# Delta rule: turning keys, queries, values and outputs with VectorE blocks and SBUF-to-SBUF DMAs instead of TensorE

## The chip, the cores and the metric

The kernel runs on one core of a Trainium2 chip. A core has a matrix engine (PE, with its weight loads as PEld), VectorE (DVE), ScalarE (ACT), GpSimd (POOL) and SyncE (SP). Each engine runs its own instructions in the order in which the program gives them, and waits in front of an instruction whose operands are not ready. SP and POOL issue the DMAs of this kernel. The metric is device time in microseconds; the kernel before took 1706.15 us, the median of three runs (1705.23 to 1707.87).

## The reference, cut to what matters

One decoder layer is computed for a prompt of 256 tokens and for 8 samples of 4 tokens, all in float32. Most of the arithmetic is in large projections (model width 2048, inner width 8192). Between them stands the gated delta rule with 8 heads of width 128, which the change is about:

```python
def l2norm(x):
    return x * lax.rsqrt(jnp.sum(x * x, -1, keepdims=True) + NORM_EPS)

qh, kh, vh = l2norm(q), l2norm(k), v            # (tokens, 8 heads, 128)
# in chunks of 64 tokens:
M    = where(strict, (k * beta) @ k.T * decay, 0)
T    = triangular_solve(eye + M, eye)
u    = T @ (v * beta)
w    = T @ (k * beta * exp(gcum))
attn = (q @ k.T) * decay
# over the chunks, with the state S (128 x 128 of each head):
v_new = u - w @ S
o     = (q * exp(gcum)) @ S + attn @ v_new
S     = S * exp(glast) + (k * exp(glast - gcum)).T @ v_new
o     = o * rsqrt(mean(o * o) + NORM_EPS) * gdn_norm_w * silu(z)
```

The samples take the same rule with chunks of 4 tokens and a given state each.

## The kernel before

**Blocks and turns.** All weights are streamed through SBUF in blocks of 512 KB. A block takes 24 matmuls: 8 weight tiles of 128 x 128, and three products each (`matmuls`, L206 to L208), since every float32 operand is split into a high and a low part. The main loop makes one turn for each block `i`, numbered from 0, and its program order is what counts below:

1. ACT writes the high part of block `i+3` (`split_hi`, L179). Its buffer is that of block `i-1`, so ACT waits here for the end of PE's matmuls of block `i-1`.
2. A generator of side work takes one step: `next(sgen)`, and then a step of the samples' generator `aux` where there is one. A `yield` in the code of the delta rule ends such a step. The step's instructions on all engines stand here in program order.
3. DVE writes the low part of block `i+3` (`split_lo`, L140, tile `lo`).
4. Pieces of evacuation that are due come next (for instance the short convolution, `w`, L265 to L287, or L318 to L334).
5. PE runs the 24 matmuls of block `i`.
6. SP issues the load of block `i+7` (`load`, L171, tile `raw`). Its buffer is free when DVE has written the low part of block `i+3`.

There are four buffers each of `raw`, `hi` and `lo`. The matmuls of block `i` need `hi` and `lo` of that block, which were written three turns earlier in program order.

**The delta rule** is side work, `gdn(G)` for the two halves `G` = 0 and 1 of four heads each; the first half begins in turn 20. For each half, keys and queries arrive with the head's width in the partitions (`kq`, `kqs` for samples). In order, `gdn` turns them by TensorE (L958, 16 transposes through the identity), sums squares for the norms (`ss`), turns the samples' keys and queries (L973, L974) and repeats the samples' keys four times (`four`, L976, then L980), computes the decays (`glx`, `gr`, L997; `E`), scales the turned keys (`kdec`), multiplies keys with keys and queries (L1030, L1031), and inverts the triangle: a small solve (`mx`, written by ACT and POOL at L1088 and L1089, used by PE at L1094), then three doublings (L1084). Then `U128`, a copy of the inverse by ACT (L1121), is ready; the values are turned by TensorE (L1219, 8 transposes) and the scan over four chunks begins (L1243, L1251, L1254, L1231). The samples run beside it (`sample`, L1139 to L1210), with repeated values at L1169 and L1176. At the end the outputs are turned (L1291, 8 transposes) and copied to `ao` by ACT.

`S0` holds the samples' states. POOL issues its loads at L926, ahead of all other work of the half. `S0` shares its place in SBUF with an earlier tile (tag `S0`).

**DMA order.** SP's DMAs are issued in program order. They take eight completion counters in turn, so that each waits for the DMA eight places before it to have landed.

## Time and profile before

| what | us |
|---|---|
| median of three runs | 1706.15 |
| span of the profiled execution | 1703.4 |
| PE busy in it | 1688.5 |
| DVE busy | 1007.2 |
| ACT busy | 734.1 |
| POOL busy | 133.8 |

The profiled execution has no time of its own beside its span; the median of the runs lies 2.75 us above that span, which holds what is before the first and after the last instruction.

The views are read in this way. A row of the waits gives the engine and line that waited, whom for, the sum in us, how often, and the longest. A row of the chain of waits, or of a timeline, starts with start and duration in us. A row of the groups ends in the sum in us, the mean in ns, and the idle time in front. A row of one source line gives least, median and greatest duration in ns. A row of the DMA issues gives the KB of one and the median time from issue to landing in us. "SPq" is SP issuing.

### The profile page before, as it was taken

The numbers are of one execution on the slowest core, as the hardware profiler recorded it, in microseconds if no ns is written. First come the engines' busy times: TensorE is split into PE (matmuls) and PEld (weight loads), VectorE is DVE, ScalarE is ACT, GpSimd is POOL, SyncE is SP. The second block draws the span as 40 slices with busy tenths as digits, with TensorE's granted clock in tenths as the row PEclk, the third lists the DMA queues.
The fourth block names the chain that finished last, engine by engine and source line by source line (L and its number), as shares of the span: only waits on it lengthen the run. The fifth ranks groups of instructions, "written<-read, shape, count | busy, mean of one in ns | idle before, by whom it ended". The sixth has DMA issues, their size and how long they took to land.

```text
span 1703.4 us, 31106 instructions
## 1 busy us (share of the span) xinstructions
PE 1688.5 (99%) x13063; PEld 1668.7 (98%) x13063; DVE 1007.2 (59%) x1296; ACT 734.1 (43%) x1067; POOL 133.8 (8%) x223
## 2 busy tenths in 40 slices
PE   9999999999999999999999999999999999999997
PEld 7999999999999999999999999999999999999997
DVE  5577876758544444456778844566445654466565
ACT  4675626333543333334445533444334433344442
POOL 2232412023300000000010000000000000000000
PEclk9999999999999999999999999999999999999999
DMA  8464456435555555555565555555555555555552
GB/s 244 140 194 139 123 175 200 150 115 180 162 170 169 166 162 170 163 164 165 158 190 174 165 170 161 164 170 162 167 168 161 163 171 162 164 167 164 162 162 80
DMA packets 275097, 279.18 MB, mean 164 GB/s; under 512 B 13131, under 2 KB 270092, under 8 KB 274952
## 3 DMA queue, kind: packets, MB, share of 16 engines
q1 hardware_dynamic: 270414, 265.95, 51.3%
q0 software_dynamic: 4256, 11.12, 2.3%
q8 instruction: 102, 1.67, 0.4%
q14 instruction: 37, 0.30, 0.1%
q10 hardware_dynamic: 288, 0.13, 0.0%
HBM read 269.68 MB, written 7.48 MB: 163 GB/s over the span
## 4 chain that ended last, share of the span: by engine, by line
PE 98%; DVE 1%; DMA 0%; POOL 0%; issue 0%; SPq 0%; ACT 0%; POOLq 0%; ACTq 0%
PE acc L206 31%; PE acc L208 31%; PE acc L207 31%; PE g L1084 1%; DMA xr<-in_x_prompt_dram 0%; PE g L1072 0%; PE g L1231 0%; PE g L1251 0%; PE g L831 0%; DVE w L143 0%; PE g L1254 0%; PE g L1203 0%; PE g L1243 0%; PE g L608 0%; PE g L798 0%; PE g L958 0%
## 5 line engine op out<-in xcount | busy, mean ns | idle before, releaser
L140 DVE TENSOR_TENSOR lo<-raw,hi 128x1024 fp32r<-128x1024 f32 (+2 forms) x502 | 614.0, 1226 | 556.2 <-ACT hi L179 553.7
L179 ACT CAST hi<-raw 128x1024 fp32r<-128x1024 f32 (+1 forms) x498 | 517.6, 1041 | 765.0 <-PE acc L207 707.7
L206 PE MATMUL acc<-xh,hi 128*128 128x288 f32 x1408 | 422.9, 300 | 0.0
L208 PE MATMUL acc<-xh,lo 128*128 128x288 f32 x1408 | 416.7, 296 | 0.0
L207 PE MATMUL acc<-xl,hi 128*128 128x288 f32 x1408 | 416.5, 296 | 0.0
L206 PE MATMUL acc<-dh,hi 128*128 128x290 f32 x1024 | 303.9, 297 | 0.0
L207 PE MATMUL acc<-dl,hi 128*128 128x290 f32 x1024 | 303.3, 296 | 0.0
L208 PE MATMUL acc<-dh,lo 128*128 128x290 f32 x1024 | 302.7, 296 | 0.0
L206 PE MATMUL acc<-hh,hi 128*128 128x288 f32 x1024 | 302.3, 295 | 0.0
L208 PE MATMUL acc<-hh,lo 128*128 128x288 f32 x1024 | 302.3, 295 | 0.0
L207 PE MATMUL acc<-hl,hi 128*128 128x288 f32 x1024 | 302.3, 295 | 0.0
L206 PEld LDWEIGHTS acc<-xh,hi 128*128 128x128 f32 x1408 | 265.4, 189 | 2.6 <-issue 0.7
L207 PEld LDWEIGHTS acc<-xl,hi 128*128 128x128 f32 x1408 | 265.8, 189 | 0.5
L208 PEld LDWEIGHTS acc<-xh,lo 128*128 128x128 f32 x1408 | 265.6, 189 | 0.0
L206 PEld LDWEIGHTS acc<-dh,hi 128*128 128x128 f32 x1024 | 193.6, 189 | 0.1
L208 PEld LDWEIGHTS acc<-dh,lo 128*128 128x128 f32 x1024 | 193.3, 189 | 0.0
L207 PEld LDWEIGHTS acc<-dl,hi 128*128 128x128 f32 x1024 | 193.3, 189 | 0.1
L207 PEld LDWEIGHTS acc<-hl,hi 128*128 128x128 f32 x1024 | 192.5, 188 | 0.0
L208 PEld LDWEIGHTS acc<-hh,lo 128*128 128x128 f32 x1024 | 192.3, 188 | 0.0
L206 PEld LDWEIGHTS acc<-hh,hi 128*128 128x128 f32 x1024 | 192.1, 188 | 0.0
L207 PE MATMUL acc<-ml,hi 128*128 128x288 f32 x256 | 75.6, 295 | 0.0
L208 PE MATMUL acc<-mh,lo 128*128 128x288 f32 x256 | 75.6, 295 | 0.0
(404 smaller groups left out, 1620.0 us busy)
## 6 DMA issues: line engine op xcount, KB each, us to landing
raw<-in_w_in_dram SPq DMA_DIRECT2D x176, 512.0 KB, 3.5
raw<-in_w_up_dram SPq DMA_DIRECT2D x128, 512.0 KB, 3.9
raw<-in_w_down_dram SPq DMA_DIRECT2D x128, 512.0 KB, 3.7
raw<-in_w_o_dram SPq DMA_DIRECT2D x32, 512.0 KB, 3.7
raw<-in_w_a_out_dram SPq DMA_DIRECT2D x16, 512.0 KB, 3.7
raw<-in_w_b_out_dram SPq DMA_DIRECT2D x16, 512.0 KB, 3.6
S<-in_state_gdn_dram POOLq DMA_DIRECT2D x8, 512.0 KB, 7.8
out_dram<-S POOLq DMA_DIRECT2D x8, 512.0 KB, 4.9
```

What stands on the lines that cost most here:

```text
L140: dve.tensor_tensor(out=out, in0=a, in1=b, op=op)
L179: act.copy(his[i][:, k:k + step], raw[i][:, k:k + step])
L206: pe.matmul(o, wh, xh_, start=st, stop=False)
L207: pe.matmul(o, wh, xl_, start=False, stop=False)
L208: pe.matmul(o, wl, xh_, start=False, stop=en)
L1084: pe.matmul(out[r, q * 64:q * 64 + 64], a[r, q, :], b[r, q, :], start=True, stop=True)
```

## The change

For each half, the 16 + 2 + 4 + 8 + 8 transposes by TensorE and the 4 products that repeat the samples' values are replaced:

- Keys, queries and the samples' keys and queries are turned in blocks of 32 x 32 within their partitions by `dve.transpose` (tiles `tk` and `ts`), and the blocks are then moved to other partitions by DMAs from SBUF to SBUF, which SP issues: 16 to `spk`, 16 to `kr` (the samples' keys repeated), 16 to `kT` and 16 to `qT`.
- The squares for the norms are taken from the moved tiles, in one piece of 1024 for keys and one for queries; `kdec` is scaled from `kT`.
- The values are turned by DVE (`tv`) and moved by 16 DMAs to `v`, ahead of the triangle's inversion. The transposes stand in a step of their own.
- `tk`, `qT`, `kT` and `tv` lie in the place of `S0`; the loads of `S0` are issued after the moves of `v`.
- The samples' values are copied by ACT (`Xs`) and repeated by 16 DMAs (`v4`).
- The outputs are turned by DVE (`to`) and moved to `ao` by 32 DMAs.
- The `yield` between the copy of `U128` and the scan is gone; two more stand in `sample`; one of two is gone ahead of the outputs' turn.

This is 128 DMAs of 8 to 32 KB for each half, all on SP's queue, between the loads of the weights.

```diff
-        S0 = pl.tile([P, 4, 8, P], F32, tag="S0", name=nm("S0"))
-        for hh in range(4):
-            gps.dma_start(S0[:, hh], A["state_gdn"][0, :, 4 * G + hh].rearrange("b d e -> d b e"))
...
-        for c in range(4):
-            kt = gtile()
-            kv = kt.rearrange("p (h c) -> p h c", h=4)
-            for hh in range(4):
-                pe.transpose(kv[:, hh, :], kq[:, hh, c].rearrange("p s x -> p (s x)"), ident)
...
-            dve.tensor_reduce(out=red[:, c, :], in_=s2, axis=mybir.AxisListType.X, op=ADD)
-            if c % 2:
+        flat = T([P, 4096], "S0")
+        tk = flat[:, 0:2048].rearrange("p (j a c r x) -> p j a c r x", j=4, a=2, c=4, r=2)
+        qT = flat[:, 2048:3072].rearrange("p (i c r x) -> p i c r x", i=4, c=4, r=2)
+        kT = flat[:, 3072:4096].rearrange("p (i c r x) -> p i c r x", i=4, c=4, r=2)
+        tv = flat[:, 0:1024].rearrange("p (j c r x) -> p j c r x", j=4, c=4, r=2)
...
+        for hh in range(4):
+            dve.transpose(out=tk[:, :, hh % 2, :, hh // 2],
+                          in_=kq[:, hh].rearrange("p c s x -> p c (s x)").rearrange("p c (j b) -> p j c b", j=4))
+            if hh == 1:
+                dve.transpose(out=ts.rearrange("p u h x -> p (u h x)"), in_=kqs.rearrange("p u h b t -> p (u h b t)"))
+            if hh % 2:
                 yield
+        for i in range(4):
+            for n in range(4):
+                sp.dma_start(spk[rows32(n), :, rows32(i)], ts[rows32(i), :, n])
+                sp.dma_start(kr[rows32(n), :, rows32(i)], ts[rows32(i), 0])
         tt(gl, bc(G_["g"][:, :, pr], 64),
            cst("lc").unsqueeze(1).unsqueeze(1).to_broadcast([P, 4, 2, 64]), MUL)
...
+        yield
+        for i in range(4):
+            for j in range(4):
+                sp.dma_start(kT[rows32(j), i], tk[rows32(i), j, j // 2])
+                sp.dma_start(qT[rows32(j), i], tk[rows32(i), j, 1 - j // 2])
         yield
...
+        for u in range(2):
+            act.activation(junk, spk[:, u], AF.Square, accum_out=ss[:, 16 + u:17 + u])
+        act.activation(sqr[:, 0:512], kr.rearrange("p h d -> p (h d)"), AF.Square)
+        dve.tensor_reduce(out=ss[:, 18:22], in_=sqr[:, 0:512].rearrange("p (h d) -> p h d", h=4),
+                          axis=mybir.AxisListType.X, op=ADD)
+        yield
+        for u, t in enumerate((kT, qT)):
+            s2 = sqr.rearrange("p (q i x) -> p i q x", q=8, i=4)
+            act.activation(s2, t.rearrange("p i c r x -> p i (c r) x"), AF.Square)
+            dve.tensor_reduce(out=ss[:, 8 * u:8 * u + 8], in_=sqr.rearrange("p (q d) -> p q d", q=8),
+                              axis=mybir.AxisListType.X, op=ADD)
         yield
...
+        while cur[0] < mark["kqv_end", G] + 3:
+            yield
+        for r in range(2):
+            dve.transpose(out=tv[:, :, :, r],
+                          in_=vf[:, r].rearrange("p c a x -> p c (a x)").rearrange("p c (j b) -> p j c b", j=4))
+        yield
+        v = T([P, 4, 4, 2, 32], "v")
+        for i in range(4):
+            for j in range(4):
+                sp.dma_start(v[rows32(j), i], tv[rows32(i), j])
+        S0 = T([P, 4, 8, P], "S0")
+        for hh in range(4):
+            gps.dma_start(S0[:, hh], A["state_gdn"][0, :, 4 * G + hh].rearrange("b d e -> d b e"))
...
+            act.copy(Xs, pv_[:, 0:P])
             act.mul(vns, pv_[:, 0:P], sc[:, 1:2])
...
+            for hh in range(4):
+                for n in range(4):
+                    sp.dma_start(v4[rows32(n), hh], Xs[rows32(hh)])
...
+        to = T([P, 4, 4, 2, 32], "kdec")
...
+        for j in range(4):
+            for i in range(4):
+                h0 = 4 * G + 1 - i // 2
+                t0 = gd["ao"][rows32(j), 1, h0:h0 + 3:2, 0:NP_].rearrange("p r (c n x) -> p n r c x", c=4, n=2)
+                for r in range(2):
+                    sp.dma_start(t0[:, i % 2, r], to[rows32(i), j, :, r])
```

How the order of the instructions moves is shown at three places, all in the first half.

SP at the first moves, before (only the loads of weights) and now. `kso` and `kr` are the moved samples' tiles (`spk` lies in the place of `kso`), `S_1125` is the flat tile with `tk`, `kT` and `qT`:

```order
L171 DMA raw_1111<-in_w_in_dram 128x4x256
L171 DMA raw_1186<-in_w_in_dram 128x4x256
L171 DMA raw_1244<-in_w_in_dram 128x4x256
L171 DMA raw_1287<-in_w_in_dram 128x4x256
L171 DMA raw_1328<-in_w_in_dram 128x4x256
```

```order
L171 DMA raw_1211<-in_w_in_dram 128x4x256
L966 DMA kso_1127<-U_1126 32x2x32
L967 DMA kr_1128<-U_1126 32x4x32
...
L171 DMA raw_1278<-in_w_in_dram 128x4x256
L973 DMA S_1125<-S_1125 32x256
L974 DMA S_1125<-S_1125 32x256
...
L171 DMA raw_1340<-in_w_in_dram 128x4x256
L171 DMA raw_1388<-in_w_in_dram 128x4x256
```

The first "..." stands for 30 more rows of the pair above it, the second for 30 more as well: 32 DMAs now stand between the loads of blocks 28 and 29 and 32 between those of blocks 29 and 30.

DVE over the same turns, now. The reductions of `ss` read squares that ACT takes from the moved tiles:

```order
L140 TENSOR_TENSOR glx_1344<-gl_1122,glx_1344 128x512
L983 TENSOR_REDUCE ss_1123<-vmh_1116 128x4
L140 TENSOR_TENSOR lo_1351<-raw_1169,hi_1342 128x1024
L143 SCALAR_TENSOR_TENSOR w_1353<-w_1353,hw 128x312 x3
L989 TENSOR_REDUCE ss_1123<-vmh_1116 128x8 x2
L140 TENSOR_TENSOR lo_1396<-raw_1211,hi_1390 128x1024
```

The two rows of `lo` are the low parts of blocks 27 and 28. They stand behind the reductions, in turns 24 and 25. Before, the reductions of `red` stood in turns 20 and 21 and that of `ss` in turn 23, each behind a square of what TensorE had turned.

POOL at the small solve, before and now. `S` is `S0`, `b` the spread keys, `mx` the operand of the small solve on PE:

```order
L273 COPY stB<-w_1588 128x27
L1065 COPY b_1120<-kqs_424 128x8x4 x4
L1089 ISA
L1089 TENSOR_TENSOR mx_1631<-xt_1538,mx_1631 128x512
L265 MEMSET w_1706 128x3
```

```order
L273 COPY stB<-w_1608 128x27
L1054 DMA S_1699<-in_state_gdn_dram 128x8x128 x4
L1075 COPY b_1115<-kqs_424 128x8x4 x4
L1099 ISA
L1099 TENSOR_TENSOR mx_1709<-xt_1558,mx_1709 128x512
L265 MEMSET w_1750 128x3
```

The four loads of `S0` have moved from the head of the half to the place just ahead of `mx`. The first of them writes where the moves of `v` read.

More of the change, by code (lines that the diff above doesn't have):

```diff
@@ L913, in gates, with rows32 @@
         yield
[L916 to L917 removed]
+    def rows32(n):
+        return slice(32 * n, 32 * n + 32)
     def gdn(G):
@@ L948, in gdn @@
         ss = T([P, 22], "ss")
-        red = T([P, 4, 4], "red")
         kdec = T([P, 4, 2, P], "kdec")
@@ L952, in gdn @@
         rows = (slice(0, 64), slice(64, 128))
-        for c in range(4):
-            kt = gtile()
-            kv = kt.rearrange("p (h c) -> p h c", h=4)
-            for hh in range(4):
-                pe.transpose(kv[:, hh, :], kq[:, hh, c].rearrange("p s x -> p (s x)"), ident)
-            s2 = sqr[:, 512 * (c % 2):512 * (c % 2) + 512].rearrange("p (h c) -> p h c", h=4)
-            act.activation(s2, kv, AF.Square)
-            for par in range(2):
-                act.copy(kdec[rows[par], c], kv[rows[par], par::2, :])
-            dve.tensor_reduce(out=red[:, c, :], in_=s2, axis=mybir.AxisListType.X, op=ADD)
-            if c % 2:
+        flat = T([P, 4096], "S0")
@@ L965, in gdn @@
                 yield
+        for i in range(4):
+            for n in range(4):
+                sp.dma_start(spk[rows32(n), :, rows32(i)], ts[rows32(i), :, n])
+                sp.dma_start(kr[rows32(n), :, rows32(i)], ts[rows32(i), 0])
         tt(gl, bc(G_["g"][:, :, pr], 64),
            cst("lc").unsqueeze(1).unsqueeze(1).to_broadcast([P, 4, 2, 64]), MUL)
-        ssv = ss[:, 0:16].rearrange("p (a c r) -> p a c r", a=2, c=4)
-        for par in range(2):
-            act.copy(ssv[rows[par], 0], red[rows[par], :, par::2])
-            act.copy(ssv[rows[par], 1], red[rows[par], :, 1 - par::2])
@@ L972, in gdn @@
-        sp2 = gtile()
-        pe.transpose(sp2[:, 0:128], kst, ident)
-        pe.transpose(sp2[:, 128:256], qst, ident)
-        gps.tensor_copy(wide, four(kst))
-        yield
-        ktr = gtile()
-        for hh in range(4):
-            pe.transpose(ktr[:, hh * P:hh * P + P], rep4[:, hh * P:hh * P + P], ident)
-        kr = T([P, 4, P], "kr")
-        for u in range(2):
-            act.activation(junk, sp2[:, u * P:u * P + P], AF.Square, accum_out=ss[:, 16 + u:17 + u])
-        act.copy(kr, ktr.rearrange("p (h d) -> p h d", h=4))
@@ L1020, in gdn @@
         act.activation(Ef, Ef, AF.Exp)
-        kdf = kdec.rearrange("p c r x -> p (c r) x")
-        tt(kdf, kdf, bc(qc(kdr), P), MUL)
+        tt(kdec.rearrange("p c r (i x) -> p i (c r) x", i=4), kT.rearrange("p i c r x -> p i (c r) x"),
+           bc(bmid(qc(kdr), 4), 32), MUL)
         yield
@@ L1168, in sample @@
             yield
-            act.copy(wide, four(Us))
             yield
@@ L1185, in sample @@
             done.append(1)
+            yield
+            yield
+            vr = sqr[:, 0:512].rearrange("p (h d) -> p h d", h=4)
+            tt(vr, v4, bc(rsc[:, 1], P), MUL)
+            v3 = pl.tile([P, 4, P], F32R, tag="U", name=nm("v3"))
+            lows(v3, vr, 1)
             vm = {}
@@ L1242, in gdn @@
             for p in range(2):
-                pe.matmul(p2[:, p * P:(p + 1) * P], U128[:, 2 * c + p, :], v[:, c, p, :], start=True, stop=True)
-            tt(v[:, c], p2[:, 0:256].rearrange("p (r x) -> p r x", r=2), bc(brk[:, c, :], P), MUL)
+                pe.matmul(ix(p2[:, p * P:(p + 1) * P]), U128[:, 2 * c + p, :], v[:, :, c, p], start=True, stop=True)
+            tt(v[:, :, c].rearrange("p i r x -> p r i x"), p2[:, 0:256].rearrange("p (r i x) -> p r i x", r=2, i=4),
+               bc(bc(brk[:, c, :], 4), 32), MUL)
             yield
@@ L1250, in gdn @@
                 r = rows[hh % 2]
-                pe.matmul(p3[hh % 2][:, hh // 2, :], kdec[r, c, hh // 2, :], v[r, c, hh // 2, :],
+                pe.matmul(ix(p3[hh % 2][:, hh // 2, :]), kdec[r, c, hh // 2, :], v[r, :, c, hh // 2],
                           start=True, stop=True)
             for p in range(2):
-                pe.matmul(p4[:, p * P:(p + 1) * P], aT[:, 2 * c + p, :], v[:, c, p, :], start=True, stop=True)
+                pe.matmul(ix(p4[:, p * P:(p + 1) * P]), aT[:, 2 * c + p, :], v[:, :, c, p], start=True, stop=True)
             p4v = p4[:, 0:256].rearrange("p (r x) -> p r x", r=2)
```

48 lines of the change are left out of this document (13 added, 35 removed).

## Prediction

> **What bounds the kernel now.** I read the page first, then the waits, then the chain that ended last.
>
> ```profile
> span 1703.4 us, 31106 instructions
> PE 1688.5 (99%) x13063; PEld 1668.7 (98%) x13063; DVE 1007.2 (59%) x1296; ACT 734.1 (43%) x1067; POOL 133.8 (8%) x223
> ACT hi L179 <- PE acc L207: 707.7, 369, 4.4
> SPq L171 <- DVE lo L140: 1373.9, 475, 9.1
> PE g L1203 <- DVE E L143: 3.0, 1, 3.0
> ```
>
> PE sets the time, and inside the program it stands still once, for 3.0 us. ACT waits for PE, SP for DVE: these run ahead of PE by three blocks and are held back by its buffers. So every matmul taken away is worth its time, and any wait that eats the lead of three blocks is paid in full. The chain gives PE's pace at the places of the change:
>
> ```profile
> 92.99 0.87 PE g L958 x8
> 97.06 0.87 PE g L958 x8
> 121.35 0.27 PE g L1030 x4
> 123.41 0.33 PE acc L206
> 139.54 0.47 PE g L1094 x2
> 180.11 0.87 PE g L1219 x8
> 201.15 0.89 PE g L1176 x8
> 279.08 0.87 PE g L958 x8
> 325.62 0.47 PE g L1094 x2
> ```
>
> Eight transposes take 0.87 us. From 93.86 to 97.06 runs block 20: 3.20 us for 24 matmuls, 0.133 each. The products of turn 28 take 2.06 (121.35 to 123.41).
>
> **What the change removes.** For each half 38 transposes, 38/8 x 0.87 = 4.1, and the repeated values, 0.89: 5.0 us, 10.0 for both. All of it is on the bounding engine and is gained. ACT's and DVE's savings gain nothing by themselves.
>
> **What it adds on SP.** Each half gets 128 DMAs in SP's queue. What an issue costs, and how long it takes to land:
>
> ```profile
> L171 SPq DMA_DIRECT2D raw<-in_w_in_dram x176: 367/368/544, 2.2 to 733.0; - x176
> L779 SPq DMA_DIRECT2D xr<-in_x_sample_dram x4: 464/465/910, 1.7 to 8.1; - x4
> 19.59 0.33 SPq L1351 DMA_DIRECT2D lnr<-in_ln_b_dram  x1
> 19.97 0.32 SPq L1352 DMA_DIRECT2D lnr<-in_gdn_norm_w_dram  x1
> L748 SPq DMA_DIRECT2D out_dram<-r x2: 717/860/1004, 1698.5 to 1699.2; - x2
> cf<-in_cf_dram SPq DMA_DIRECT2D x1, 64.0 KB, 2.0
> out_dram<-Y SPq DMA_DIRECT2D x4, 256.0 KB, 2.7
> xr<-in_x_sample_dram SPq DMA_DIRECT2D x4, 64.0 KB, 8.9
> ```
>
> A 512 KB load costs SP 0.37 us and a half-KB one 0.32, so size hardly matters; from 19.59 to 19.97 one follows the other with 0.05 between. No SBUF-to-SBUF DMA is in this trace. Bounds: 0.37 us for each (0.32 + 0.05), and 0.51 (0.465 + 0.05, `xr` from L779, the same 32 partitions); 0.86 was seen where two queues issued at once. I take 0.41, the steady load and the gap. Landing: 2.0 is the least, 2.7 for stores out of SBUF, 8.9 at the crowded start. I take 2.0, the nearest in size. So 32 moves hold SP for 13.1 us, 16 for 6.6, and a moved tile lands 2 us behind its last issue.
>
> [...]
>
> Other durations:
>
> ```profile
> L179 ACT CAST hi<-raw 128x1024 fp32r<-128x1024 f32 x492 | 514.2, 1046 | 761.7 <-PE acc L207 707.7 <-issue 41.4 <-ACT hi L179 8.6
> L140 DVE TENSOR_TENSOR lo<-raw,hi 128x1024 fp32r<-128x1024 f32 x492 | 608.7, 1239 | 552.6 <-ACT hi L179 550.2
> L963 DVE TENSOR_REDUCE red<-vmh 128x4 f32<-128x512 f32 x8 | 5.5, 686 | 8.2 <-ACT vmh L960 8.2
> L1114 DVE STREAM_TRANSPOSE xt<-U 128x512 f32<-128x512 f32 x4 | 2.8, 712 | 0.1
> L140 DVE TENSOR_TENSOR kdec<-kdec,kdr 128x1024 f32<-128x1024 f32 x2 | 2.4, 1215 | 0.0
> 117.13 0.29 DVE L1001 RECIPROCAL rn<-nr 128x22 f32<-128x22 f32 x1 [1.26 <-ACT nr L1000]
> ...
> 118.88 0.69 DVE L140 TENSOR_TENSOR E<-E,cf 128x512 f32<-128x512 f32 x1
> ...
> 122.91 0.68 DVE L140 TENSOR_TENSOR gl<-E,nbr 128x512 f32<-128x512 f32 x1
> ...
> 125.09 1.39 DVE L140 TENSOR_TENSOR aT<-g,E 64x512 f32<-64x512 f32 x2
> ...
> 127.65 1.70 DVE L143 SCALAR_TENSOR_TENSOR w<-w,hw 128x312 f32<-128x312 f32 x3
> ```
>
> So: `hi` 1.05, `lo` 1.24, a reduction of 512 0.69 and of 1024 about 1.2 (`lo`, of equal size), two turned tiles of 512 1.42, `kdec` 1.2, the group from `rn` to `E` 2.44 (117.13 to 119.57), from `gl` to `aT` 3.57 (122.91 to 126.48), the convolution 1.70.
>
> **First half, the moves of keys.** Turn 20 starts at 93.0 as before; without transposes turns 21 to 25 start 3.20 apart, 96.2 to 109.0.
>
> - Turn 21: `hi` to 97.3, two turned tiles behind the convolution to 98.5, `lo` to 99.7, then SP's load to 100.1. The 32 moves of turn 22 end 13.1 later at 113.2; the last, issued at 112.8, lands at 114.8. The load of block 29 ends at 113.6. The 32 moves of keys and queries end at 126.7; the last of the keys is issued at 125.9 and lands at 127.9, the queries 0.4 later, hidden.
> - Turn 24: ACT squares `kr` (0.6) to 115.4, DVE reduces to 116.1, the low part of block 27 follows at 117.3. PE has started turn 27 at 115.9 (112.2 + 0.47 of L997 + 3.20) and wants the low part after two matmuls, at 116.2: it stops for 1.1.
> - Turn 25: square of keys 1.05, reduction 1.2, square of queries into the same scratch 1.05, reduction 1.2, then the low part of block 28, 1.24: 127.9 + 5.8 = 133.7. PE starts turn 28 at 120.2, does 2.06 of products and two matmuls, and stops at 122.5: 11.2 us.
> - Turns 29 to 33: DVE is now what PE follows. Its low parts are ready at 139.1 (1.70 + 2.44 + 1.24), 141.5, 146.3 (3.57 + 1.24), 149.2 and 153.6 (1.70 + 1.42 + 1.24); PE's turns start at 136.7, 142.0, 145.2, 149.2, 152.4: it stops for 2.1, 0, 0.8, 0 and 0.9.
>
> The late loads of blocks 29 and 30, queued behind the moves, land by 117.2 and 130.7 and are not what is late.
>
> **First half, the small solve.** POOL's rows:
>
> ```profile
> 85.66 3.60 POOL L926 DMA_DIRECT2D S<-in_state_gdn_dram  x4
> 128.32 2.25 POOL L1065 COPY b<-kqs 128x32 f32<-128x32 f32 x4
> 135.91 1.55 POOL L1089 TENSOR_TENSOR mx<-xt,mx 128x512 fp32r<-128x512 f32 x1 [5.34 <-ACT mx L1088]
> ```
>
> In turn 31 SP's 16 moves of `v` follow the load at 154.0; the last is issued at 160.2 and lands at 162.2. POOL's first load of `S0` waits for that, since `tv` lies there. Behind it on POOL stand three more loads, the copies and `mx`: 3.6 + 1.7 (four copies, 2.25 in this row beside a busy DVE, so I take less) + 1.55 gives 169.1. PE comes to the small solve, turn 34, at 156.5 and stops for 12.6. Before, the loads of `S0` waited for nothing and were issued long ahead; this cover is gone.
>
> The half's stops: 1.1 + 11.2 + 2.1 + 0.8 + 0.9 + 12.6 = 28.7.
>
> **Second half.** It starts one turn earlier, behind the 32 moves of the outputs, which hold SP until 5.9 us after its start; with three loads behind them the first moves begin at 7.5. `kr` lands at 22.2, `kT` at 35.3. The convolutions are missing on DVE. The same steps give low parts at 25.0 (block +7, PE wants it at 23.1), 41.0 (+8, wanted at 30.3), then stops of 0.6 and 0.6; `v` lands at 64.5, `mx` is ready at 70.9, and PE is there at 61.3. Stops: 1.9 + 10.7 + 0.6 + 0.6 + 9.6 = 23.4.
>
> **The missing step ahead of the scan.** ACT's copy of `U128` and PE's first product with it now stand in one turn:
>
> ```profile
> 180.01 1.05 ACT L179 CAST hi<-raw 128x1024 fp32r<-128x1024 f32 x1 [2.39 <-PE acc L207]
> 180.96 1.24 ACT L1121 COPY U<-U 64x512 f32<-64x512 f32 x2
> ```
>
> PE is free at 180.11 and the copy ends at 182.20: 2.1 us of standing for each half, 4.2.
>
> **PE's pace after a long stop.** At the start of the trace matmuls follow each other more slowly:
>
> ```profile
> 11.02 0.66 PE L798 MATMUL g<-cf,xr 128*128 128x128 f32 x2 [0.45 <-DMA xr<-in_x_prompt_dram]
> ...
> 19.47 0.44 PE L207 MATMUL acc<-xl,hi 128*128 128x288 f32 x1
> 19.71 0.44 PE L208 MATMUL acc<-xh,lo 128*128 128x288 f32 x1
> ```
>
> 0.24 against 0.133, and this holds from PE's last stop at 11.02 until 19.95 at least: 8.9 us of which 8.9 x (1 - 0.133/0.24) = 4.0 are lost. Whether a stop of ten us brings that back, no row shows; the bounds are 0 and 4.0 for each long stop. After the moves of keys it costs nothing, since DVE and POOL set what follows. After the small solve I take the middle, 2 us for each half, 4 in all. [...]
>
> **Costed at nothing.** The 16 moves of `v4` (6.6 + 2.0) have two turns and more than 8 us until `vr`. The moves of outputs delay one weight load by 13 us; it has 7 us until ACT wants it and 7 more until PE does. New strides of the scan's operands move the same elements. The stop of 3.0 at L1203 may go or grow, as POOL's order changes: 3 either way.
>
> **The sum.** -10.0 + 28.7 + 23.4 + 4.2 + 4 = +50.3. The span becomes 1703.4 + 50.3 = 1753.7; the median of the runs lies 2.75 above the profiled span, so **1756 us**.
>
> The bounds: 80 issues lie on each half's two chains, 160 in all; at 0.37 they give -6, at 0.51 +16. Six landings at 2.7 give +4. The pace gives -4 or +4, L1203 -3 or +3. The likeliest case's own range is 1743 to 1783.
>
> **The rivals.**
>
> - *Cheap issues: faster.* If an SBUF-to-SBUF move cost SP at most 0.1 us, 64 would take 6.4, the keys would land at 108 and all low parts would be in time; POOL would have `mx` 13.1 us after the start of turn 30 (2.6 to the load, 1.6 + 2.0, 3.6, 1.7, 1.55), just as PE comes. Then only -10.0 + 4.2 is left, 1700 us. It decides from about 0.2 us: 127.9 - 11.2 = 116.7 is when the keys must land. Against it: no issue of SP in these rows is under 0.32. [...] 6%.
> - *Only the keys' moves bite.* If the moves of `v` land and POOL gets through before PE comes, the stops of 12.6 and 9.6 and the 4 of pace fall away: 1730. For it: POOL's rows are rough, and its first load might be let go by the first of the moves that free its place; against it, it would have to come 12.6 us sooner. 13%.
> - *Slow moves.* With eight in flight, a landing of 5 us sets a pace of 5/8 = 0.63: 160 x 0.22 + 6 x 3 = 53 more, about 1809. For it: the 8.9 of the crowded start and the 0.86 of L748; against it, both rows are of moments when many DMAs stood in line, and 64 KB landed in 2.0. 9%.
>
> **How the numbers follow.** The forecast holds 70%; 2% remain for a change that cancels to nothing. Predicted 1756, range 1728 to 1785: it takes in the second rival and leaves out the first and the third and what lies past the bounds. A measurement of this kernel tells 0.2% (3.4 us) from no change. Faster: 8% (the first rival, and some unseen gain); same 3%; slower 89%.
>
> **What would show it.** Right: SP's moves at 0.37 to 0.51 a piece; DVE's `ss` waiting for ACT and ACT for DMA by ten us; PE's longest waits at L208 for `lo` and at the small solve for POOL's `mx`, some 10 us each, twice; 2 us at the first product of the scan. Wrong: moves issued in 0.1 us, or PE busy through turn 28, or `mx` ready before PE.

## The result, and the profile after

The changed kernel takes **1829.7 us** (median of four runs, 1828.8 to 1830.2) against 1705.7 for the kernel before beside it: a ratio of 1.072, 95% interval 1.0704 to 1.0735. The sign was forecast, the size was not: 1756 was predicted, and 1829.7 lies 45 us above the range. The profiled execution has a span of 1828.4, 125.0 more than before and 74.7 more than the sum of the prediction (1753.7).

The page of the changed kernel, its span, PE, and PE's granted clock in 40 slices:

```profile
span 1828.4 us, 31220 instructions
PE 1703.5 (93%) x12971; PEld 1677.5 (92%) x12971; DVE 1013.1 (55%) x1308; ACT 724.2 (40%) x1029; POOL 128.0 (7%) x221
PEclk9987999868998999999999999999999999999999
```

PE stands for 6% of the span, and in the slices of the delta rule the clock falls to 0.6 to 0.8, where all slices of before show 9. Its waits, with the sum, the number and the longest, in us:

```profile
PE acc L208 <- DVE lo L140: 41.6, 8, 16.2
...
PE g L1250 <- ACT U L1131: 4.3, 2, 2.1
PE g L1250 <- DVE v L143: 2.5, 6, 1.1
```

All rows of this view add up to 117.4 us, against 7.1 before: 110.3 us of new stops. Eight of them are long. In the timeline of PE (start, duration, instruction; in brackets how long PE had stood, and for whom):

```profile
126.41 0.61 PE L208 MATMUL acc<-xh,lo 128*128 128x288 f32 x1 [10.11 <-DVE lo L140]
148.56 0.61 PE L206 MATMUL acc<-xh,hi 128*128 128x288 f32 x1 [15.41 <-ACT w L268]
187.75 0.80 PE L1104 MATMUL g<-mx,bo 128*128 128x512 f32 x1 [14.14 <-POOL mx L1099]
...
350.49 0.61 PE L206 MATMUL acc<-xh,hi 128*128 128x288 f32 x1 [10.23 <-ACT hi L179]
...
373.84 0.61 PE L208 MATMUL acc<-xh,lo 128*128 128x288 f32 x1 [12.62 <-DVE lo L140]
398.04 0.61 PE L208 MATMUL acc<-xh,lo 128*128 128x288 f32 x1 [16.21 <-DVE lo L140]
431.65 0.80 PE L1104 MATMUL g<-mx,bo 128*128 128x512 f32 x1 [12.12 <-POOL w L318]
572.10 0.61 PE L206 MATMUL acc<-xh,hi 128*128 128x288 f32 x1 [9.84 <-ACT hi L179]
```

The first three are the first half: behind the 32 moves to `spk` and `kr`, behind the 32 of keys and queries, and at the small solve. The next four are the second half, the first of them behind the first half's 32 output moves. The last stands behind the second half's output moves. Each is longer than forecast, or was not forecast. The way from the moves to the first two stops of a half is the forecast one: ScalarE's squares wait for the moves (L981 for the keys' row copy `kr` and `kso`, L988 for keys and queries), and VectorE's sums and the low parts `lo` stand behind them. ScalarE's waits, the sum, number and longest over both halves:

```profile
ACT vmh L988 <- DMA S<-S: 37.7, 2, 19.3
ACT vmh L981 <- DMA kso<-U: 32.0, 2, 16.5
```

Why they are longer stands in the rows of SP's issues, one source line each (least, median and greatest duration of one issue in ns):

```profile
L171 SPq DMA_DIRECT2D raw<-in_w_in_dram x176: 367/368/796, 2.2 to 857.8; - x176
L966 SPq DMA_DIRECT2D kso<-U x32: 585/599/1673, 100.5 to 368.6; - x32
L1051 SPq DMA_DIRECT2D v<-S x32: 512/589/1562, 169.8 to 423.6; - x32
L1304 SPq DMA_DIRECT2D ao<-kdec x64: 585/599/1615, 323.4 to 566.2; - x64
```

A load of weights costs SP 0.37 us in the median as before, though one right behind moves took 0.53 (at 122.39). A move from SBUF to SBUF costs 0.59 to 0.60, with the 0.05 to the next one **0.64 us**, where the prediction took 0.41. It landed 1.8 to 1.9 us after its issue, where the prediction took 2.0.

The second difference is PE's pace. Windows of PE in the changed kernel (width, PE's busy time with the number of matmuls begun, granted clock, DMA share, GB/s), each 8 us from the end of a long stop:

```profile
148.60:156.60 8.00, 6.52 (x33) 0.68 0.25 74
187.75:195.75 8.00, 8.00 (x48) 0.78 0.78 221
...
398.00:406.00 8.00, 7.96 (x44) 0.70 0.49 138
```

The clock is 0.68 to 0.78, and 33 to 48 matmuls are begun in 8 us. What is left of the span's growth, 125.0 - 110.3 + 10.0 = 24.7 us, I put down to this pace. It is a remainder, not a measurement: summed over PE's busy time up to 600 us, the granted clock falls short of 1.0 by 20.7 us, so that some 21 of the 24.7 are shown and the other 3 to 4 stay open.

### The profile page after: what moved, and what is told of

The parts are those of the page before. It is cut to its first block, busy times and chain, and to the rows that moved or that the text cites. A ratio compares the mean times of both kernels' runs of the same rounds, so it can differ in the third digit from the quotient of the medians.

```text
span 1828.4 us, 31220 instructions
## 1 busy us (share of the span) xinstructions
PE 1703.5 (93%) x12971; PEld 1677.5 (92%) x12971; DVE 1013.1 (55%) x1308; ACT 724.2 (40%) x1029; POOL 128.0 (7%) x221
## 3 DMA queue, kind: packets, MB, share of 16 engines
q0 software_dynamic: 4256, 11.12, 2.2%
## 4 chain that ended last, share of the span: by engine, by line
PE 81%; SPq 8%; DVE 4%; DMA 2%; issue 2%; POOL 1%; ACT 1%; POOLq 0%; DVEq 0%; ACTq 0%
PE acc L206 26%; PE acc L207 26%; PE acc L208 26%; SPq L1304 2%; DVE lo L140 2%; DMA raw<-in_w_in_dram 1%; SPq L1051 1%; SPq L974 1%; SPq L1187 1%; SPq L966 1%; SPq L973 1%; SPq L967 1%; PE g L1094 1%; DMA xr<-in_x_prompt_dram 0%; PE g L1082 0%
## 5 line engine op out<-in xcount | busy, mean ns | idle before, releaser
L208 PE MATMUL acc<-xh,lo 128*128 128x288 f32 x1408 | 425.0, 302 | 41.7 <-DVE lo L140 41.6
L206 PE MATMUL acc<-xh,hi 128*128 128x288 f32 x1408 | 429.9, 305 | 35.5 <-ACT hi L179 20.1
L207 PE MATMUL acc<-xl,hi 128*128 128x288 f32 x1408 | 423.5, 301 | 0.0
L208 PEld LDWEIGHTS acc<-xh,lo 128*128 128x128 f32 x1408 | 272.5, 194 | 44.1 <-DVE lo L140 44.1
L206 PEld LDWEIGHTS acc<-xh,hi 128*128 128x128 f32 x1408 | 273.1, 194 | 38.5 <-ACT hi L179 20.5
L206 PE MATMUL acc<-dh,hi 128*128 128x290 f32 x1024 | 303.9, 297 | 0.0
L206 PE MATMUL acc<-hh,hi 128*128 128x288 f32 x1024 | 302.3, 295 | 0.0
L207 PEld LDWEIGHTS acc<-xl,hi 128*128 128x128 f32 x1408 | 273.1, 194 | 0.6
L206 PEld LDWEIGHTS acc<-dh,hi 128*128 128x128 f32 x1024 | 193.6, 189 | 0.1
L206 PEld LDWEIGHTS acc<-hh,hi 128*128 128x128 f32 x1024 | 192.1, 188 | 0.0
```

What stands on the lines that cost most here:

```text
L206: pe.matmul(o, wh, xh_, start=st, stop=False)
L207: pe.matmul(o, wh, xl_, start=False, stop=False)
L208: pe.matmul(o, wl, xh_, start=False, stop=en)
```

## The experiments

**The theory** after this reading: (1) SP needs 0.64 us for each move, and what stands behind the moves on SP (weight loads) or waits for them (ACT, DVE, POOL's loads of `S0`) is late by their sum; (2) each such stop costs about 2.5 us more by a slower clock behind it, 24.7 over ten stops (the eight, and two of 2.1 at L1250). **The rivals**: the moves were slow because many stood in line, or because the DMA engines were full; the chain of keys was late by ACT's and DVE's work; the pace had its cause in the transfers.

### What an issue costs

The kernel before, with nine groups of six DMAs between scratch tiles, one group each in a turn of the up-projection.

```diff
+                if n == 0:
+                    sp.dma_start(dst[:, c], src[:, c])
+                elif n == 1:
+                    sp.dma_start(dst[0:64, c], src[64:128, c])
+                elif n == 2:
+                    sp.dma_start(dst[q, c], src[r, c])
...
+                elif n == 4:
+                    sp.dma_start(dst[q, 32 * k:32 * k + 32], src[r, 32 * k:32 * k + 32])
+                elif n == 5:
+                    sp.dma_start(dst[r, c], W[0:32, c])
+                elif n == 6:
+                    sp.dma_start(dst[:, c], W[0:128, c])
+                elif n == 7:
+                    act.dma_start(dst[q, c], src[r, c])
+                else:
+                    gps.dma_start(dst[q, c], src[r, c])
```

> The kernel before with nine probes in the up-projection, each of six DMAs in one turn between scratch tiles (nothing of the computation is left out): SyncE moving 128 partitions within SBUF, 64, 32 onto other partitions, 32 onto the same ones (all of 1 KB runs), 32 with 128 B runs, 32 and 128 partitions loaded from HBM, then the 32-partition move issued by ScalarE and by GpSimd. Theory (an SBUF-to-SBUF move costs SyncE more to issue than a load, whatever its run): 0.55 to 0.60 us for each of the first five, 0.37 for the two loads. Rival 1 (few partitions cost, not the source): 0.37 for the 128-partition move and load, 0.59 for all of 32 partitions, the load too. Rival 2 (the moves of the changed kernel were slow because so many stood in line): 0.37 to 0.41 for all, six being few. Landings: 1.8 to 2.0 us for all SBUF moves.

The rows of the lines, in the order of the diff (the two left out, 64 partitions and 32 onto the same ones, have medians of 525 and 550):

```profile
L1388 SPq DMA_DIRECT2D scr<-scr x6: 465/528/601, 1058.3 to 1064.7; - x6
L1392 SPq DMA_DIRECT2D scr<-scr x6: 572/589/593, 1109.3 to 1112.5; - x6
L1396 SPq DMA_DIRECT2D scr<-scr x6: 515/590/591, 1160.6 to 1163.7; - x6
L1398 SPq DMA_DIRECT2D scr<-in_w_up_dram x6: 310/390/952, 1186.2 to 1192.4; - x6
L1400 SPq DMA_DIRECT2D scr<-in_w_up_dram x6: 327/328/498, 1211.7 to 1218.7; - x6
L1402 ACTq DMA_DIRECT2D scr<-scr x6: 594/608/624, 1237.7 to 1240.9; - x6
L1404 POOL DMA_DIRECT2D scr<-scr x6: 498/498/514, 1242.3 to 1245.1; - x6
```

All five kinds of SBUF-to-SBUF DMA on SP have medians of 0.53 to 0.59, whether 128, 64 or 32 partitions and with runs of 1 KB or 128 B; the loads from HBM have 0.33 and 0.39. So a move from SBUF to SBUF costs here some 0.2 us more than a load of the same shape (0.53 against 0.33 with 128 partitions, 0.59 against 0.39 with 32), and rival 1 falls: the move of 128 partitions has 0.53 and not 0.37, the load of 32 has 0.39 and not 0.59. What is left of a difference between the moves goes with how close the issues stand: the two rows whose six start within 3.1 and 3.2 us have medians of 0.59, the three whose six are spread over 6.1 to 6.5 us have 0.53 to 0.55, with leasts of 0.46 to 0.51. Six in a turn cost each as much as 32 in line (1109.3 to 1112.5 is five steps of 0.64), so rival 2 falls as far as the length of the line goes. ScalarE issued a move in 0.61, GpSimd in 0.50 (medians).

Why a move from SBUF to SBUF costs SP more, these rows don't tell. The source alone does not make it: in the kernel before, stores from SBUF to HBM (`out_dram<-Y`) took 0.36 and 0.37 after a pause, 0.43 to 0.73 directly behind another. The landings of the probe's moves had medians of 1.9 to 3.7 us, with the weights' loads beside them; 1.8 to 2.0 was forecast.

### What a stop costs beside itself

The kernel before, with six stops of PE in the up-projection: a product, a copy by ScalarE, then `n` fills by GpSimd, and a product that waits for them. No DMA is in it.

```diff
+            pe.matmul(t[:, 0:P], ones, pa[:, 0:P], start=True, stop=True)
+            act.copy(pa[:, 128:256], t[:, 0:P])
+            gps.tensor_copy(pa[:, 256:384], pa[:, 128:256])
+            for _ in range(n):
+                gps.memset(pa, 0.0)
+            t = gtile()
+            pe.matmul(t[:, 0:P], ones, pa[:, 0:P], start=True, stop=True)
```

> The kernel before with six stops of TensorE in the up-projection, 20 turns apart: a small product that waits for 1, 2, 4, 6, 9 and 14 fills of a scratch tile by GpSimd, no DMA in it (nothing of the computation is left out). Theory (a long stop by itself slows TensorE afterwards, which is where 25 us of the changed kernel's loss lie): after the shortest stops, up to some 2 us, a block takes its 3.2 us again; after those of 6 us and more the granted clock falls below 1.0 and the blocks of the next 5 to 15 us lose 2 to 5 us per stop. Rival (the slow stretches came from the moves, or from the other engines' lateness): a clock of 1.0 and blocks of 3.2 us behind every stop.

The stops were 3.3, 4.4, 6.7, 8.9, 12.2 and 17.8 us. Windows of PE as above, 8 us from the end of each stop, first this kernel:

```profile
1061.60:1069.60 8.00, 7.99 (x49) 0.79 0.19 61
...
1205.80:1213.80 8.00, 8.00 (x40) 0.62 0.00 0
...
1445.70:1453.70 8.00, 7.95 (x43) 0.68 0.59 173
```

and a window of the kernel before:

```profile
1061.60:1069.60 8.00, 8.00 (x63) 1.00 0.63 188
```

Behind the six stops 49, 45, 40, 43, 45 and 43 matmuls are begun in 8 us instead of 62 or 63: on average 18 fewer, 18 x 8.0/62.5 = 2.3 us lost by each stop. The clock is 0.50 to 0.54 in the first 2 us and 1.00 in the next window of 8 us. The loss does not grow with the stop in this run: 17.8 us cost as much as 4.4 (43 and 45 matmuls). With no DMA of the stop's own the rival falls, since the slow stretches of the changed kernel (0.68 to 0.79) look the same.

From what length? The same kernel with shorter stops:

```diff
-            gps.tensor_copy(pa[:, 256:384], pa[:, 128:256])
-            for _ in range(n):
-                gps.memset(pa, 0.0)
+            if w:
+                gps.memset(pa[:, 256 - w:256] if w < 256 else pa[:, 0:w], 0.0)
```

> The kernel before with six stops of TensorE in the up-projection, 20 turns apart, shorter than those of the earlier probe: a product, ScalarE's copy of it, a fill by GpSimd of 0, 128, 448, 768, 1152 and again 0 elements a partition, and a product that waits for them; some 1.0 to 2.4 us each (nothing of the computation is left out). Theory 1 (there is a length below which a stop costs only itself; the 2.1 us stops of the changed kernel at the scan lay below it): clock 1.0 and no fewer products in the microseconds behind each. Theory 2 (every stop is followed by half pace): 8 to 10 products instead of 17 in the 2 us behind each, as behind the stops of 3.3 us and more, some 2 us lost each.

The stops were 0.9, 1.3, 1.5, 1.7, 2.1 and 0.9 us. Windows of 1 us behind those of 1.7 and 2.1:

```profile
1262.80:1263.80 1.00, 1.00 (x9) 1.00 0.98 305
...
1328.60:1329.60 1.00, 1.00 (x8) 0.73 0.70 187
1329.60:1330.60 1.00, 1.00 (x6) 0.50 0.90 298
...
1332.60:1333.60 1.00, 1.00 (x10) 1.00 1.03 157
```

Up to 1.7 us a stop of this run costs itself, with a clock of 1.00 in all windows behind it. The one of 2.1 brings the half clock too, a microsecond after PE has gone on, for some 3 us. So neither theory holds as put: the step lies between 1.7 and 2.1 in this run, and both stops of 2.1 at the scan of the changed kernel bring the half clock (0.51 from 477.9 to 480.9 behind the second). A window of the changed kernel behind the first of these:

```profile
233.00:236.00 3.00, 3.00 (x16) 0.57 0.00 0
```

But no one length decides. A stop of 3.0 us, at L1203, stands in the kernel before and, at the same place, in the kernels of the probes. A window of 1 us soon behind it, first in the kernel before, then in that of the issues' probe:

```profile
217.80:218.80 1.00, 1.00 (x10) 1.00 0.00 0
217.90:218.90 1.00, 1.00 (x6) 0.50 0.06 16
```

The clock's own record says what differs here. In the profile of the changed kernel, the granted clock falls to 0.50 ten times between 25 and 600 us, for 3.41 to 17.07 us each, and all its changes lie multiples of 3.41 us apart. Take the windows of 3.41 us that these changes mark, and count in each that ran at full clock how long PE stood. In the window ahead of each of the ten falls PE stood for 63% or more (at the two stops of 2.1, for 2.15 of 3.41 us). In six windows it stood for 20 to 38%, and half clock followed none of them. In the kernel before, windows counted back from the one change of its record, at 1696.42, put the stop of 3.0 across two: it fills 36% of one (211.62 to 215.03) and 51% of the next, and the clock stays at 1.00. So in these two profiles what counts is how much of one window a stop fills, and a stop of 3.0 us that falls across two passed. The six stops of 3.3 us and more of the probe and the eight long ones of the changed kernel each brought half clock.

### The mask behind the states' loads

The changed kernel with the loads of `S0` behind POOL's part of `mx`.

```diff
-        for hh in range(4):
-            gps.dma_start(S0[:, hh], A["state_gdn"][0, :, 4 * G + hh].rearrange("b d e -> d b e"))
...
         gps.tensor_tensor(out=mx[:, 1], in0=Xf, in1=mx[:, 0], op=SUB)
+        for hh in range(4):
+            gps.dma_start(S0[:, hh], A["state_gdn"][0, :, 4 * G + hh].rearrange("b d e -> d b e"))
```

> The changed kernel with the four loads of the samples' states issued by GpSimd behind the mask of the small solve instead of ahead of it. Theory (the small solve waits for a mask that stands behind loads that wait for the values' sixteen moves): the stops of 14.1 and 12.1 us at the small solve go, and some 3 us of slow pace behind each: 1798 us (1793 to 1808). Rival (the values' moves hold up the work wherever they stand, and the weights' loads behind them stop TensorE instead): 1820 to 1830.

1813.4 us (1811.9 to 1817.0), ratio 1.0625, interval 1.0608 to 1.0643: 16 less than the changed kernel, between the two. POOL's timeline in this kernel:

```profile
172.97 1.52 POOL L1097 TENSOR_TENSOR mx<-xt,mx 128x512 fp32r<-128x512 f32 x1 [12.15 <-ACT mx L1096]
182.13 3.60 POOL L1099 DMA_DIRECT2D S<-in_state_gdn_dram  x4 [7.64 <-DMA v<-S]
185.71 0.13 POOL L265 MEMSET w<- 128x3 f32 x1
```

The mask is ready at 174.5 instead of 187.7, and the stops of 14.1 and 12.1 shrink to 1.1 at most. But POOL still stands until 182.1 in front of loads that wait for the moves of `v`; behind them now stand the convolution's copies (L265, L266), ACT waits for these, and PE for ACT, 5.0 us. The theory named the right wait; what it missed is that the queue was emptied of only one of its customers.

### The outputs by TensorE

The changed kernel with the outputs turned as before.

```diff
-        for j in range(4):
-            for i in range(4):
...
-                for r in range(2):
-                    sp.dma_start(t0[:, i % 2, r], to[rows32(i), j, :, r])
+        for u in range(2):
+            pt = gtile()
+            for w in range(4):
+                pe.transpose(pt[:, w * P:(w + 1) * P], of[:, 4 * u + w, :], ident)
```

> The changed kernel with the outputs turned by TensorE and copied by ScalarE as before, without the 32 output moves of each half. Theory (32 moves of 0.64 us are 20.6 us of SyncE and outrun the 14 us by which the weights' loads are ahead): the stops of 10.2 and 9.8 us go, with 2 to 5 us of pace behind each, and 1.7 us of TensorE come back: 1829.7 - 20.0 - 7 + 1.7 = 1804 us (1801 to 1808). Rival (those stops are only the earlier ones' lateness handed on): they stay, 1829 to 1832.

1802.4 us (1802.0 to 1804.3), ratio 1.0566, interval 1.055 to 1.0582: as the theory had it. Both stops of L206 for `hi` are gone from the waits. So the 64 output moves, costed at nothing, cost 27 us, and that is net of the 1.7 us that TensorE's turns cost in their place. Part of it lies in the second half's keys: the first stop for `lo` there falls from 12.6 to 8.2, so the first half's output moves had held up the second half's key moves too.

### Fewer moves, and moves on another queue

First, the changed kernel without the queries' moves; then, with `kr` and `qT` moved by POOL.

```diff
-                sp.dma_start(qT[rows32(j), i], tk[rows32(i), j, 1 - j // 2])
...
-        for u, t in enumerate((kT, qT)):
+        for u, t in enumerate((kT, kT)):
```

```diff
-                sp.dma_start(kr[rows32(n), :, rows32(i)], ts[rows32(i), 0])
+                gps.dma_start(kr[rows32(n), :, rows32(i)], ts[rows32(i), 0])
...
-                sp.dma_start(qT[rows32(j), i], tk[rows32(i), j, 1 - j // 2])
+                gps.dma_start(qT[rows32(j), i], tk[rows32(i), j, 1 - j // 2])
```

> The changed kernel without the sixteen moves of the queries in each half; the norms of the queries are taken from the keys, so that part of the computation is changed, all the rest is done. Theory (each move costs SyncE 0.64 us, and the weights' loads behind them are late by their sum): 16 x 0.64 = 10.2 us less of stops in each half, all stops still long enough for a slow stretch behind them: 1829.7 - 20.5 = 1809 us (1803 to 1814). Rival (the chain of keys is late because of a landing, or because of VectorE's and ScalarE's work on the moved tiles, not because of the number of moves): 1822 or more.

> The changed kernel with the repeated keys' moves and the queries' moves issued by GpSimd instead of SyncE, 32 of the 64 of each half that stand ahead of the small solve. Theory (SyncE's issuing is the limit, and GpSimd issues such a move in 0.56 us, as the probe showed): SyncE's 41 us of key moves per half become 20.5, the stops of this chain shrink from 27 and 29 us to 7 to 9 us: 1829.7 - 41 - 4 = 1785 us (1778 to 1800). Rival 1 (GpSimd's own work waits behind its moves, the convolution's copies above all, and stops TensorE in SyncE's place): 1800 to 1820. Rival 2 (the DMA engines are the limit, whichever engine issues): 1820 or more.

Without the queries' moves: 1814.1 us (1813.8 to 1815.9), ratio 1.0633, interval 1.0619 to 1.0648. The stop of 15.4 in the first half becomes 4.6, and those of the second half for `lo` fall from 28.8 to 20.3: 10.8 and 8.5, near 16 x 0.64. The time fell by 15.6, 5 us less than forecast. All stops together fell by 18.7; the other 3 us are pace. The granted clock falls short of 1.0 by 23.4 us of PE's busy time up to 600 us, where the changed kernel has 20.7. One place is a stop of 1.4 us at 265.9 with short ones beside it: 42 matmuls are begun in the 8 us behind it, against 53 behind the stop of 1.1 at this place of the changed kernel, where the clock is 1.00.

Half on POOL: 1794.2 us (1793.1 to 1794.9), ratio 1.0514, interval 1.05 to 1.0528: 35.5 less, in the theory's range. Its waits of PE:

```profile
PE g L1104 <- POOL mx L1099: 14.7, 1, 14.7
...
PE acc L208 <- DVE lo L140: 10.9, 5, 5.4
PE acc L206 <- ACT w L268: 6.9, 1, 6.9
```

The key chains' stops (the rows for `lo` and for `w` L268) are 17.8 together instead of 57.0; the other large ones are within 1.5 us of what they were. The moved bytes left SP's queue for POOL's own (11.12 MB on it in the changed kernel, 12.70 here). The 16 DMA engines, on which the profile counts both queues, were busy for 0.38 of the time from 122 to 160 us in the changed kernel, and for 0.44 here, so these were not the limit: it was how fast SP's queue takes DMAs up, 0.64 us a move. Whether SP itself or what serves its queue sets that pace, this run does not separate.

### The step ahead of the scan

```diff
         tt(vq, vq, bc(bmid(nr[:, 0:8], 4), 32), MUL)
+        yield
```

> The changed kernel with the scan's first product one turn later, so that ScalarE's copy of the inverse and VectorE's scaling of the values stand a turn ahead of it. Theory: the two stops of 2.1 us go and nothing else moves: 1829.7 - 4.2 = 1825.5 us (1823.5 to 1827.5). Rival (a stop of this size slows TensorE behind it too, 2 us each): 1821 to 1822.

1823.8 us (1821.2 to 1825.2), ratio 1.0686, interval 1.0672 to 1.0701: 5.9 less. Of the rows for L1250, 6.8 us with the six short waits for `v`, 0.2 is left, and one stop of 3.5 for `vm` came at L1215, with half clock of its own behind it (1.00 from 225 to 245 us, but 0.98 over 230 to 300). The time lies in the theory's range, but the spread of 4 us between runs and the new stop leave theory and rival apart by too little to decide here; the clock of 0.57 behind the stop that went speaks for the rival.

### The same moves, four in a turn

This goes out from the kernel before: only the values, the samples' values and the first half's outputs are turned by DVE and moved, never more than four moves in a turn; keys, queries and the second half's outputs stay with TensorE, and `S0` is loaded early as before.

```diff
+    def moves(pairs_, per):
+        for k in range(0, len(pairs_), per):
+            for d, t in pairs_[k:k + per]:
+                sp.dma_start(d, t)
+            yield
...
+        tv = T([P, 4, 4, 2, 32], "vml")
...
+        aux.append(moves([(v[rows32(j), i], tv[rows32(i), j]) for i in range(4) for j in range(4)], 4))
...
+            yield from moves([(v4[rows32(n), hh], Xs[rows32(hh)]) for hh in range(4) for n in range(4)], 4)
...
+            late.append(moves(ds, 4))
```

> The kernel before, with only those turns of its blocks done by VectorE and moves that have time: the values (16 moves a half), the samples' values (16 a half) and the first half's outputs (32), never more than four moves in a turn, the values' tile ahead of the scan by nine turns; keys, queries and the second half's outputs stay with TensorE. Theory (a move costs nothing as long as SyncE gets through a turn's moves and load, 4 x 0.64 + 0.41 = 2.97 us, within the turn's 3.2 us): no new stop, and 32 small products and transposes of some 0.11 us less on TensorE: 1706.2 - 3.5 = 1702.7 us (1701.5 to 1704). Rival (moves hold up the weights' loads even so, or the VectorE work collides): 1706 or more, with waits on the loads or on VectorE in the trace.

**1699.9 us** (1699.8 to 1701.4) against 1706.2: ratio 0.9965, interval 0.9951 to 0.9978. It beats both kernels, by 0.35% the one before, and lies 1.6 us below the theory's range. SP's timeline while the values move:

```profile
153.83 2.42 SPq L925 DMA_DIRECT2D v<-vml  x4
156.35 0.53 SPq L171 DMA_DIRECT2D raw<-in_w_in_dram  x1
156.92 2.41 SPq L925 DMA_DIRECT2D v<-vml  x4
```

Four moves and a load take 3.09 us (153.83 to 156.92), just under a turn's 3.2, though the load between moves takes 0.53 there and not 0.37. PE has no wait for a load. Of the 5.4 us by which the span is shorter (1698.0), PE's busy time gives 3.2, near the forecast's 3.5; the rest is mostly fewer stops, 5.1 in all instead of 7.1: the one of 3.0 at L1203 is gone, and one of 1.4 at L1257 is new.

The same moves in bursts:

```diff
-        aux.append(moves([(v[rows32(j), i], tv[rows32(i), j]) for i in range(4) for j in range(4)], 4))
+        aux.append(moves([(v[rows32(j), i], tv[rows32(i), j]) for i in range(4) for j in range(4)], 16))
...
-            late.append(moves(ds, 4))
+            late.append(moves(ds, 32))
```

> The spread kernel with the same moves in bursts: the values' 16 in one turn, the samples' values' 16 in one turn, the first half's outputs' 32 in one turn. Theory (a burst is free up to the some 14 us by which the weights' loads are ahead, at 0.64 us a move): 16 moves are 10.2 us and cost nothing, 32 moves are 20.5 us and stop TensorE for 6 to 10 us, with 2.2 us of half pace behind: 1699.9 + 8 to 12 = 1710 us (1707 to 1713). Rival 1 (any burst stops TensorE by what it takes beyond one turn): 1725 or more. Rival 2 (bursts don't matter, spreading did nothing): 1700 to 1702.

1717.9 us (1715.1 to 1719.7), ratio 1.0067, interval 1.005 to 1.0083: 18 us more than the spread kernel, between the theory and its first rival. Its waits of PE:

```profile
PE acc L206 <- ACT hi L179: 5.4, 1, 5.4
PE g L1094 <- ACT xt L1127: 2.4, 2, 2.2
```

and one of ACT's, which the spread kernel has not:

```profile
ACT hi L179 <- DMA raw<-in_w_in_dram: 29.7, 5, 15.1
```

The 32 output moves stop PE for 5.4 us, just under what was forecast. The bursts of 16 are not free: behind them PE stands 2.2 us for ACT's copies in the inversion, and 1.8 for `vm`. ACT waits for late loads and does its other work behind them, so a load can be in time for PE and still be too late for something behind it on ACT. The clock is below 1.0 behind the two longer stops (0.94 and 0.91 over 30 and 40 us), which is the rest.

### The keys' moves alone

The changed kernel, with values, samples' values and first outputs spread as above, the second half's outputs by TensorE, `S0` loaded ahead of the values; the 64 key and query moves of each half as they were. The edit also takes over the spread kernel's step ahead of the scan and the values' own tile.

```diff
+        S0 = T([P, 4, 8, P], "S0")
+        for hh in range(4):
+            gps.dma_start(S0[:, hh], A["state_gdn"][0, :, 4 * G + hh].rearrange("b d e -> d b e"))
         kkp, kqp = gtile(), gtile()
```

> The changed kernel with only its keys' and queries' moves as they were (64 of them in two turns of each half); the values', the samples' values' and the first half's outputs' moves go four a turn, the second half's outputs are turned by TensorE, and the states' loads stand ahead of the values. Theory (the rest costs nothing when it is spread, and 64 moves in two turns are 41 us of SyncE against some 14 us by which the loads are ahead): the stops of the two key chains stay, 27 and 24 us, with 2.2 us of half pace behind each of some five long stops, and TensorE has 6.5 us less than in the spread kernel: 1699.9 - 6.5 + 51 + 11 = 1755 us (1748 to 1766). Rival (the chain of keys alone costs little; it is the values' moves and the mask behind them): 1730 or less.

1771.1 us (1766.4 to 1778.4), ratio 1.0382, interval 1.0353 to 1.041: 5 us above the range. The second half's stops for `lo` were 31.9 instead of 24, and 5.7 more came at the small solve. The expectation had counted the spread moves as free, but those of the first half's outputs were still under way: sixteen stood on SP ahead of the second half's key moves, four between the two groups of these, and twelve right behind. So, with all outputs by TensorE:

```diff
-            late.append(moves(ds, 4))
...
-        for u in range(2 * G):
+        for u in range(2):
```

> As the run before it on the keys, with the first half's outputs turned by TensorE too, so that no output move stands among the second half's key moves (16 of them did there, ahead of the keys' and between their two groups, and the second half lost 44 us in three stops, where the changed kernel lost 29). Theory: 64 key moves cost each half the same, some 24 to 27 us of stops with two or three stretches of half pace: 1771 - 20 + 1 - 3 = 1749 us (1744 to 1757). Rival (the second half's key chain costs more than the first's for another reason, the states' loads or the mask): 1765 or more.

1761.8 us (1761.3 to 1763.8), ratio 1.0328, interval 1.0311 to 1.0345. Its waits of PE:

```profile
PE acc L208 <- DVE lo L140: 36.3, 6, 16.8
PE acc L206 <- ACT w L268: 15.4, 1, 15.4
```

26.6 us stand in the first half and 24.8 in the second: the two halves cost the same, as the theory had it. The time is 5 us above the range by a fault in the expectation: its 44 us counted one stop of 12.1 twice, across the edge of two windows. With 31.9 in its place the same sum gives 1761. So the keys' moves alone, with the gains of the rest, cost 55 us against the kernel before, not the 24 of the second rival.

## Why the prediction was right or wrong

- **What bounds the kernel**: right. PE's time counts, and stops are paid in full; behind 620 us PE is busy throughout in both kernels.
- **The stops of the keys' moves, 1.1 + 11.2 and 1.9 + 10.7**: the places and the mechanism held, the size did not. Measured 10.1 + 15.4, and 12.6 + 16.2. Of the two stops of each half, the first was forecast near zero, since at 0.41 us `kr` and the loads behind its moves came almost in time.
- **The step that failed first: "I take 0.41, the steady load and the gap"**, and with it the bound of 0.51. A move costs 0.64 with the gap. Over the 160 issues of the chains that is 160 x 0.23 = 36.8 us more. The stops of the two halves, without those behind outputs, are 42.0 and 41.9 against 28.7 and 23.4: 31.8 more. The rows used were all DMAs with HBM on one side; the probe shows that a move from SBUF to SBUF costs some 0.2 us more than a load (0.59 against 0.39 with 32 partitions). The row nearest in kind (32 partitions) was no bound for it. The row left out as a crowd, 0.86 for `out_dram<-r`, was the only issue cited with an SBUF source.
- **Landing 2.0**: right (1.8 to 1.9). The third rival was wrong in its cause: its pace of 0.63 a move is near the 0.64 that came, but by issues, not by slow landings.
- **The small solve waiting for POOL behind `S0`, 12.6 and 9.6**: right; 14.1 and 12.1, and moving the loads took both away. (By the first half's steps the second half's `mx` would come at 71.3 where the prediction has 70.9, 0.4 us that decide nothing.)
- **The missing step ahead of the scan, 4.2**: right; 4.3. It had a companion in the short waits for `v` (2.5), and half clock behind both stops, which the prediction did not count.
- **"The moves of outputs delay one weight load by 13 us; it has 7 us until ACT wants it and 7 more until PE does"**: the second step that failed. They delay it by 20.5, and PE stood 10.2 and 9.8 us. Even the cover was smaller than 14: 20.5 less 10 is 10.5. In the bursts' kernel 32 moves stopped PE for only 5.4. The cover depends on how far ahead the loads are at that place; what sets it there stays open.
- **PE's pace, 2 us at the small solve and nothing at the keys**: the third step that failed. The mid value was right for one stop (2.3 in the probe), but such a loss came behind ten stops, not two: 24.7 instead of 4, of which the clock's record shows some 21. The argument that at the keys "DVE and POOL set what follows" did not hold: the blocks behind those stops ran at a clock of 0.68 to 0.79 and were late by it.
- **What was removed, 10.0**: the spread kernel confirms the unit, 3.2 of 3.5 us for its share.
- **`v4`, strides**: nothing, as costed; no wait of PE names them.
- **The 2.75 us between span and median**: set the median of three runs against the span of another run. In the runs of the changed kernel, each time lies 1.8 to 2.2 us above its own span. The forecast would have been 1755.5, less than 1 us away.

In sum, from 1753.7 to 1828.4: 31.8 in the two chains, 20.4 behind the outputs, 20.7 of pace, 1.8 elsewhere.

## What to carry to other kernels

Count DMA issues like instructions: a queue that also carries the loads of a bound engine has a budget of issues in each turn (here four moves of 0.64 and a load in 3.2 us). Moves within that budget bought 0.35%, and moves in blocks of 16 to 64 cost from 0.7% (the bursts) to 7% (the changed kernel, with all that waited behind them). Take an issue's price from a row of the same kind of DMA, with the same memories on both sides and standing as close behind another issue; where there is none, let the range reach to the dearest row that comes near. In the probe, the stops of the matrix engine of 3.3 to 17.8 us each brought the half clock and cost 2.3 us on average beside themselves. Of the shorter ones, 2.1 us brought it and 1.7 did not, and 3.0 did in one profile and not in another. So count stops as well as adding them up.

## What the runs showed of the hardware that was not expected

- In the probe of issues, an SBUF-to-SBUF DMA took SP 0.53 to 0.59 us to issue (medians, from 4 KB to 128 KB; least 0.46), a load from HBM with 32 and 128 partitions 0.39 and 0.33. GpSimd took 0.50 for such a move there and 0.50 to 0.55 in the run with half of the moves on POOL, ScalarE 0.61.
- In the profile of the changed kernel, the granted clock of TensorE changes on a grid of 3.41 us: the ten windows at full clock with PE idle for 63% or more were each followed by half clock, the six with 20 to 38% were not.
- The half clock of TensorE cost the same behind a stop of 4.4 us as behind one of 17.8 (45 and 43 matmuls begun in 8 us, 62 or 63 at full clock). In the longest stop of the probe it set in 2 to 3 us after the last product and ended 5 us after work went on:

```profile
1429.70:1430.70 1.00, 0.00 (x0) 0.85 0.09 31
1430.70:1431.70 1.00, 0.00 (x0) 0.50 0.65 122
...
1449.70:1450.70 1.00, 1.00 (x6) 0.50 0.92 251
1450.70:1451.70 1.00, 1.00 (x9) 0.91 0.70 172
```

- 54 DMAs added in the up-projection, six in a turn, left the time where it was (1706.0 against 1706.2): there SP had that much room.
